# Expert stage of a two-layer diffusion backbone: routing tables, normed rows and final gathers moved

## The chip, the cores and the metric

The kernel runs on one core of one Trainium2 chip. The metric is the device time of one launch in microseconds (us). Before the change three runs gave 2681.62, 2683.39 and 2692.31 us; the median, 2683.39 us, is the time before.

## What is computed

The reference is a two-layer backbone over 512 latent tokens and 256 context tokens, with 1024 channels in fp32. Each layer has a modulated RMSNorm, four token mixers, an output projection with a gated residual, then a second modulated norm and a feed-forward part. The change touches the feed-forward part of the last layer, which sends each token to two of eight experts:

```python
h2 = rms_norm(x_lat, norm2_g) * (1.0 + sc2) + sh2
logits = h2 @ router
top_val, top_idx = lax.top_k(logits, 2)
gates = jax.nn.softmax(top_val)
out = sum over e of combine[..., e] * ((silu(h2 @ w1[e]) * (h2 @ w3[e])) @ w2[e])
x_lat = x_lat + g2 * out
return rms_norm(x_lat, final_norm_g)
```

An expert is 1024 to 1408 to 1024. Only the 512 latent tokens take part, so there are 1024 token-expert pairs.

## The kernel before

The program is traced in Python; a compile-time scheduler then fixes each engine's order, with the traced order as priority. An engine works strictly in its fixed order. Matrix products are made from fp32r parts: an operand is split into a high part (a ScalarE copy, L259) and a low part (a VectorE subtraction, L260), and `mm3` (L272 to L274) adds three products.

**Output projection with the router beside it.** The mixers' end multiplies by w_out in eight column tiles m. For the last layer `moe_begin` first loads the router and a table of constants (`mc`), and with `spread` (L319, L320: eight TensorE transposes and two ScalarE copies) lays the norm's scale `Ar` and the gate `g2r` out as rows. Then `moe_add` (L1640) makes each tile of the new x, and `moe_x` (L1643 on) adds to the sum of squares, adds to the router's logits and turns the tile into rows of tokens: x into `xt`, x times `Ar` into `hm`.

**`moe_route` (L1658 on).** From the sum of squares it takes each token's 1/rms, `rs`. ScalarE scales the four 128-row parts of `hm` by `rs` (L1677) and SP writes them to the DRAM tensor `hd` (L1678); SP also writes `xt` to `xq` (L1675). VectorE ranks the logits, counts tokens per expert and orders the experts by count, so that the three largest get two blocks of 128 tokens each ("wide") and the other five one block ("narrow"): NB = 11 blocks, and NOV = 4 more that are run only if a count overflows. The table of which token stands in which row of which block, `inv`, is written at L1765. After it stand the results' tables: the gates by way of an Exp on ScalarE (L1785), `gr` (each block row's gate, L1799 to L1801), `rowE` and `rowL` (where each token's two results will lie, L1812, L1813), and for the last block `li` and `g7` (token numbers, the other result's row, gate; L1848 to L1851). Their temporaries lie in the pool `mh`, whose space the expert stage takes over once it is closed.

**`moe_run` (L1854 on).** Two lanes share the stage: lane 0 has the three wide experts, lane 1 the five narrow ones. Each expert has 11 steps f, one for each 128 columns of the hidden layer, so lane 0 has 33 steps, lane 1 has 55, and 88 in all. A step loads 1.5 MB of weights on SP's queue into three buffers `rawm` and two `rawv`, splits them on ScalarE and VectorE, and multiplies: `first` makes silu(w1)*w3, and `second`, one step later in the order, adds its product with w2 to the block's result in PSUM. A wide step has 48 products of 256 columns and 12 of 512, a narrow one 24 and 6. The order of the steps is written out by hand:

```python
order = sorted(((i + 0.5) / len(t) * (0.87 if early and n == 0 else 1), n, *x) for n, t in enumerate(todo) for i, x in enumerate(t))
```

With 0.87 the wide lane ends early and the last seven steps are narrow, all of the last block (NB - 1). The first step is narrow, the second wide. POOL gathers a block's rows from `hd` by `inv` (`fetch`, L1864); `rows_in` turns them by eight transposes a block (L1877) in two PSUM tiles, and from each it makes four pairs of 128x128: ScalarE adds the shift `mB` and takes the high part (L1881), VectorE adds the shift and takes the low part (L1882). At f == 10 a block's result is multiplied by `gr` and `g2r` (L1938) and written by POOL to `yb` (L1939). The PSUM tag `sml`, with two buffers, serves the products of `first` and the transposes.

**The end.** Seven steps before the end `early` is traced: POOL gathers by `rowE` and `li` from `yb` with an add (L1970), four parts of `xt` twice and then the last block's rows `x7` (a tile `xr`) twice, and `norm_out` squares, normalizes and writes the four parts (L1977 to L1983). `final` does the same for the last block's own rows after the last product (L2016 to L2025). After that the overflow count is read and the conditional part is skipped when it is zero.

Of the kernel before, what the change touches and what calls it, by code (L numbers as in the profile page):

```python
# [11 lines left out]
F32 = mybir.dt.float32  # L12
# [210 lines left out]
class Ker:  # L223
# [1385 lines left out]
    def moe_begin(s, l, wp):  # L1609

        E, V, S, mh, mod = s.E, s.V, s.S, s.mh, s.mods[l]
        s.rt = mh.tile([128, KT, 8], F32, name="router")
        s.mc = mh.tile([128, 349], F32, name="mcst")
        s.Q.dma_start(s.rt, s.I['router'])
        s.Q.dma_start(s.mc, s.I['mcst'])
        A = mh.tile([128, KT], F32, name="mA")
        V.scalar_tensor_tensor(A, mod[:, 32:40, 0], 1.0, s.prm[:, l, P_N2:P_N2 + 8], op0=OP.add, op1=OP.mult)
        s.RA = mh.tile([128, KT, 8], F32, name="RA")
        V.tensor_mul(s.RA, s.rt, A[:, :, None].to_broadcast([128, KT, 8]))
        s.Ar = wp.tile([128, D], F32, name="Ar")  # L1620
        s.mB = mod[:, 24:32, 0]
        for dst, src in ((s.Ar, A), (s.g2r, mod[:, 40:48, 0])):
            s.spread(dst, src, s.tx)
        ps = s.tx()
        for k in range(KT):
            E.matmul(ps[:, :8], mod[:, 24 + k, 0:1].to_broadcast([128, 128]), s.rt[:, k], start=k == 0, stop=k == KT - 1)
        s.bR = mh.tile([128, 8], F32, name="bR")
        V.tensor_copy(s.bR, ps[:, :8])
        s.ltr, s.onr = (mh.tile([128, 128], F32R, name=n) for n in ("ltr", "onr"))
        V.tensor_copy(s.ltr, s.mc[:, 72:200])  # L1630
        V.tensor_copy(s.onr, s.ones)
        s.hm = mh.tile([128, 4, D], F32, name="hm")
        s.lgt = s.ps("lgt")
# [8 lines left out]
    def moe_x(s, m, wp):  # L1642

        x = s.xl[m]
        s.sumsq(m, LAT, wp, x)
# [9 lines left out]
    def moe_route(s, wp):  # L1655
# [15 lines left out]
        lg = tp.tile([128, 4, 8], F32, name="lg")  # L1671
        V.tensor_mul(lg, ps[:, :32].rearrange("p (a b) -> p a b", a=4), rs[:, :, None].to_broadcast([128, 4, 8]))
        V.tensor_add(lg, lg, s.bR[:, None].to_broadcast([128, 4, 8]))
        for j in range(4):
            s.Q.dma_start(s.xq[128 * j:128 * j + 128], s.xt[j])  # L1675
        for j in range(4):
            S.activation(s.hm[:, j], s.hm[:, j], AF.Copy, scale=rs[:, j:j + 1])  # L1677
            s.Q.dma_start(s.hd[128 * j:128 * j + 128], s.hm[:, j])  # L1678
# [11 lines left out]
        rk = tp.tile([128, 4, 8], F32, name="rk")  # L1690
# [11 lines left out]
        cnt = tp.tile([128, 1, 8], F32, name="cnt")  # L1702
        V.tensor_copy(cnt[:, 0], pq[:, :8])
        er = tp.tile([128, 1, 8], F32, name="er")
# [8 lines left out]
        w = tp.tile([128, 8, 8], F32, name="ew")  # L1713
# [26 lines left out]
        rf = tp.tile([128, 2, 4], F32, name="rf")  # L1740
        one = [tp.tile([128, 4, 8], F32, name=f"one{i}") for i in range(2)]
# [7 lines left out]
        ge = tp.tile([128, 8, 17], F32, name="ge")  # L1749
        V.tensor_tensor(ge, rr[:, :, None].to_broadcast([128, 8, 17]), mc[:, None, 200:217].to_broadcast([128, 8, 17]), OP.is_ge)  # L1750
        pl = tp.tile([128, 8], F32, name="pl")
# [6 lines left out]
        ohp = tp.tile([128, 8, 128], F32R, name="ohp")  # L1758
# [18 lines left out]
        V.tensor_copy(s.regv, ef[0:1, 8:13])  # L1777

# [12 lines left out]
        gh, gl = (tp.tile([128, 8, 2, 16], F32R, name=f"g{n}") for n in "hl")  # L1791
        gh, gl = gh[:, :, 0], gl[:, :, 0]
# [4 lines left out]
        pg = s.tx()  # L1797
# [48 lines left out]
        p7 = s.tx()  # L1846
# [6 lines left out]
    def moe_run(s, lanes, wp, early=None, final=None):  # L1853
# [14 lines left out]
        def rows_in(blocks, xrs):  # L1868
# [4 lines left out]
            for i, xr in enumerate(xrs):  # L1873
                for q in range(2):
                    ps = s.sml()
                    for k in range(4):
                        E.transpose(ps[:, 128 * k:128 * k + 128], xr[:, 512 * q + 128 * k:512 * q + 128 * k + 128], s.idn)  # L1877
                    for k in range(4):
                        o = (slice(None), 4 * q + k, slice(128 * i, 128 * i + 128))
                        pk, m = ps[:, 128 * k:128 * k + 128], s.mB[:, 4 * q + k:4 * q + k + 1]  # L1880
                        S.activation(a[o], pk, AF.Identity, bias=m)  # L1881
                        V.scalar_tensor_tensor(c[o], pk, m, a[o], op0=OP.add, op1=OP.subtract)  # L1882
# [60 lines left out]
        order = sorted(((i + 0.5) / len(t) * (0.87 if early and n == 0 else 1), n, *x) for n, t in enumerate(todo) for i, x in enumerate(t))  # L1943
# [5 lines left out]
        for at, (_, n, j, f) in enumerate(order):  # L1949
# [15 lines left out]
            if early and at == len(order) - 7:  # L1965
                early()
# [18 lines left out]
    def moe(s):  # L1985
# [6 lines left out]
        with s.pool("pr", 1, PSUM) as s.pp:  # L1992
            s.nsml = 2
            with s.pool("mw") as wp:
                fo = wp.tile([128, 8], F32, name="fos")

                def early():
# [29 lines left out]
                s.moe_run([[(expert(j), [2 * j, 2 * j + 1]) for j in range(3)], [(expert(j), [3 + j]) for j in range(3, 8)]], wp, early, final)  # L2027
# [6 lines left out]
            with s.tc.If(nov > 0):  # L2034
# [5 lines left out]
                with s.pool("fin") as fp:  # L2040
# [3 lines left out]
                    s.norm_out(fp, fp.tile([128, 4], F32, name="fss"))  # L2044
# [39 lines left out]
```

## Time and profile before

| | |
|---|---|
| median of three runs | 2683.39 us |
| the profiled execution's own time | 2689.9 us |
| its span, first to last instruction | 2688.1 us |
| TensorE busy | 2423.1 us, 90% |
| VectorE, ScalarE, POOL busy | 62%, 46%, 18% |
| transfers | 327.73 MB, 122 GB/s over the span |

The profile gives one execution's instructions. Busy time of TensorE is pipelined, so that a full row need not be the engine's peak. PEclk is the TensorE clock that was granted, as a share of 2.4 GHz: 1.00 and 0.50 are its two levels. "DMA share" is the busy share of the core's 16 DMA engines. A timeline row has start, duration, engine, line and operands (out<-in), and in brackets the idle time before it with what ended it. "Landing" is the time from a transfer's issue to its data's arrival.

### The profile page before, as it was taken

What the parts mean: (1) busy time and instruction counts of PE and PEld (TensorE: products, weight loads), DVE (VectorE), ACT (ScalarE), POOL (GpSimd) and SP (SyncE); (2) the same over time, 40 slices, a digit from 0 to 9 for tenths busy, and PEclk for the clock granted to TensorE, in tenths of its full rate; (3) what the DMA queues carried; (4) which work ended last, traced back from release to release, by engine and by line L of the source; (5) the groups of instructions that cost most, each with busy time, mean ns of one, the idle gap of its engine ahead of it and who ended that gap; (6) DMA issues with size and microseconds to landing.
All of it is one profiled execution on the core that took longest, in us unless ns stands there. A gap on an engine that the chain in (4) does not pass through costs nothing. (4 is left out here: it accounts for less than half of the span.)

```text
span 2688.1 us, 46555 instructions
## 1 busy us (share of the span) xinstructions
PE 2423.1 (90%) x18148; PEld 2005.0 (75%) x18148; DVE 1661.6 (62%) x3158; ACT 1240.9 (46%) x2396; POOL 483.9 (18%) x619
## 2 busy tenths in 40 slices
PE   7999788879988999999999998888995989999993
PEld 3889666656677888888887876765674979988882
DVE  5573698877497544343355738876635676667673
ACT  3373366546623211212234726754734565655552
POOL 1010454541020000000120025653011000000011
PEclk9999898999999999999999999999996999999996
DMA  6233100011054434343411320001126877878785
GB/s 239 75 96 112 50 25 27 22 64 56 24 169 153 128 104 126 112 131 126 130 44 60 94 71 2 25 27 47 40 66 223 266 255 247 263 235 267 235 280 159
DMA packets 162037, 327.73 MB, mean 122 GB/s; under 512 B 12400, under 2 KB 84848, under 8 KB 161808
## 3 DMA queue, kind: packets, MB, share of 16 engines
q1 hardware_dynamic: 153600, 294.65, 34.1%
q0 software_dynamic: 8208, 30.02, 3.6%
q8 instruction: 145, 2.38, 0.4%
q14 instruction: 84, 0.69, 0.1%
HBM read 296.97 MB, written 26.21 MB: 120 GB/s over the span
## 5 line engine op out<-in xcount | busy, mean ns | idle before, releaser
L272 PE MATMUL big<-hhi,hiw 128*128 128x512 f32 (+1 forms) x1504 | 519.4, 346 | 8.1 <-ACT hhi L491 3.5
L273 PE MATMUL big<-hlo,hiw 128*128 128x512 f32 (+1 forms) x1504 | 521.5, 347 | 2.4 <-DVE hlo L492 2.4
L274 PE MATMUL big<-hhi,low 128*128 128x512 f32 (+1 forms) x1504 | 517.7, 344 | 5.6 <-DVE low L260 3.9
L259 ACT CAST hiw<-raww 128x512 fp32r<-128x512 f32 (+3 forms) x208 | 158.4, 769 | 612.4 <-PE big L273 408.2
L272 PEld LDWEIGHTS big<-hhi,hiw 128*128 128x128 f32 x1504 | 285.0, 190 | 52.4 <-ACT hhi L491 5.4
L274 PEld LDWEIGHTS big<-hhi,low 128*128 128x128 f32 x1504 | 284.5, 189 | 45.2 <-DVE low L260 5.6
L273 PEld LDWEIGHTS big<-hlo,hiw 128*128 128x128 f32 x1504 | 285.2, 190 | 41.3 <-DVE hlo L492 4.2
L260 DVE TENSOR_TENSOR lom<-rawm,him 128x1024 fp32r<-128x1024 f32 x176 | 214.9, 1224 | 128.6 <-ACT him L259 126.5
L260 DVE TENSOR_TENSOR low<-raww,hiw 128x512 fp32r<-128x512 f32 (+3 forms) x196 | 177.1, 908 | 158.2 <-ACT hiw L259 157.9
L259 ACT CAST him<-rawm 128x1024 fp32r<-128x1024 f32 x176 | 183.9, 1046 | 149.0 <-PE sml L273 63.9
L272 PE MATMUL sml<-xh,him 128*128 128x256 f32 x528 | 154.0, 292 | 0.2
L273 PE MATMUL sml<-xl,him 128*128 128x256 f32 x528 | 151.7, 287 | 0.0
L274 PE MATMUL sml<-xh,lom 128*128 128x256 f32 x528 | 151.5, 287 | 0.0
L272 PE MATMUL sml<-him,xh 128*128 128x256 f32 x440 | 129.0, 293 | 10.0 <-DVE xl L1882 9.0
L260 DVE TENSOR_TENSOR lov<-rawv,hiv 128x1024 fp32r<-128x1024 f32 x88 | 107.5, 1221 | 47.4 <-ACT hiv L259 46.0
L273 PE MATMUL sml<-lom,xh 128*128 128x256 f32 x440 | 127.2, 289 | 0.0
L274 PE MATMUL sml<-him,xl 128*128 128x256 f32 x440 | 127.0, 289 | 0.0
L273 PE MATMUL big<-gl,hiw 128*128 128x512 f32 (+1 forms) x352 | 119.5, 339 | 0.0
L259 ACT CAST hiv<-rawv 128x1024 fp32r<-128x1024 f32 x88 | 92.2, 1048 | 58.5 <-PE y L274 48.4
L272 PE MATMUL big<-gh,hiw 128*128 128x512 f32 (+1 forms) x352 | 118.9, 338 | 0.0
L274 PE MATMUL big<-gh,low 128*128 128x512 f32 (+1 forms) x352 | 118.2, 336 | 0.0
L757 POOL TENSOR_TENSOR Gm<-G,mskf 128x256 f32<-128x256 f32 x120 | 98.9, 832 | 82.3 <-PE a L612 79.0
(610 smaller groups left out, 5676.8 us busy)
## 6 DMA issues: line engine op xcount, KB each, us to landing
rawm<-in_m SPq DMA_DIRECT2D x176, 512.0 KB, 5.1
rawv<-in_m SPq DMA_DIRECT2D x88, 512.0 KB, 5.0
raww<-in_wadt SPq DMA_DIRECT2D x56, 512.0 KB, 3.5
raww<-in_w SPq DMA_DIRECT2D x52, 512.0 KB, 3.9
raww<-in_winc SPq DMA_DIRECT2D x92, 256.0 KB, 3.0
raww<-in_wout SPq DMA_DIRECT2D x16, 512.0 KB, 4.2
wadt<-in_wadt SPq DMA_DIRECT2D x16, 512.0 KB, 4.3
raww<-in_w SPq DMA_DIRECT2D x16, 448.0 KB, 3.3
```

The source lines that it names most:

```text
L259: s.S.copy(hi, src)
L260: (eng or s.V).tensor_sub(lo, src, hi)
L272: s.E.matmul(out, ah, bh, start=start, stop=False)
L273: s.E.matmul(out, ah, bl, start=False, stop=False)
L274: s.E.matmul(out, al, bh, start=False, stop=stop)
L757: P.tensor_mul(x, G[:, :, 0, :, 0], s.mskf[:, 1 - d, i][:, None, None].to_broadcast(sh))
```

## The change

- `hd` is filled with the shift `sh2` before the rows exist: in `moe_begin` the buffer `g2r` holds the spread shift first, and SP writes it to the four parts of `hd`. In `moe_route` the scaled `hm` is added to `hd` by four POOL transfers with `accum_op=add`; the four writes of `xq` are traced after them. The gate is spread into `g2r` later, in `moe_x` at m == 4.
- `rows_in` no longer adds the shift: one ScalarE copy and one VectorE subtraction for 128x512 take the place of four pairs of 128x128.
- The results' tables become `moe_tables`, traced as a hook after step 2 of the 88, with their PSUM from `sml`; the tiles that they read or make are moved to the pool `mo`, which stays open.
- The wide lane's factor is 0.8, so that eleven narrow steps are last. The gathers (`sums`) are traced eleven steps before the end, with `x7`'s gather after the four of each round; `norm_out` is split: the squares (`norm_rms`) three steps before the end, two parts of the output two steps before, and two one step before.

```diff
-        s.mc = mh.tile([128, 349], F32, name="mcst")
+        s.mc = s.mo.tile([128, 349], F32, name="mcst")
...
-        s.mB = mod[:, 24:32, 0]
-        for dst, src in ((s.Ar, A), (s.g2r, mod[:, 40:48, 0])):
+        for dst, src in ((s.Ar, A), (s.g2r, mod[:, 24:32, 0])):
             s.spread(dst, src, s.tx)
+
+        for j in range(4):
+            s.Q.dma_start(s.hd[128 * j:128 * j + 128], s.g2r)
...
+        if m == 4:
+            s.spread(s.g2r, s.mods[1][:, 40:48, 0], s.tx)
...
         for j in range(4):
+            S.activation(s.hm[:, j], s.hm[:, j], AF.Copy, scale=rs[:, j:j + 1])
+            P.dma_start(s.hd[128 * j:128 * j + 128], s.hm[:, j], accum_op=OP.add)
+        for j in range(4):
             s.Q.dma_start(s.xq[128 * j:128 * j + 128], s.xt[j])
-        for j in range(4):
-            S.activation(s.hm[:, j], s.hm[:, j], AF.Copy, scale=rs[:, j:j + 1])
-            s.Q.dma_start(s.hd[128 * j:128 * j + 128], s.hm[:, j])
 
         def rank(dst, x, n):
...
-        ohp = tp.tile([128, 8, 128], F32R, name="ohp")
+        ohp = s.mo.tile([128, 8, 128], F32R, name="ohp")
...
+        s.tab = lg, one, ge, pl, ohp, rf, er, cnt, u
+
+    def moe_tables(s):
+
+        E, V, S, tp, mc = s.E, s.V, s.S, s.mo, s.mc
+        lg, one, ge, pl, ohp, rf, er, cnt, u = s.tab
+        y = tp.tile([128, 4, 8], F32, name="yl")
...
-        pg = s.tx()
+        pg = s.sml()
...
-                    for k in range(4):
-                        o = (slice(None), 4 * q + k, slice(128 * i, 128 * i + 128))
-                        pk, m = ps[:, 128 * k:128 * k + 128], s.mB[:, 4 * q + k:4 * q + k + 1]
-                        S.activation(a[o], pk, AF.Identity, bias=m)
-                        V.scalar_tensor_tensor(c[o], pk, m, a[o], op0=OP.add, op1=OP.subtract)
+                    pv = ps.rearrange("p (a b) -> p a b", a=4)
+                    o = (slice(None), slice(4 * q, 4 * q + 4), slice(128 * i, 128 * i + 128))
+                    s.split(a[o], c[o], pv)
...
-        order = sorted(((i + 0.5) / len(t) * (0.87 if early and n == 0 else 1), n, *x) for n, t in enumerate(todo) for i, x in enumerate(t))
+        order = sorted(((i + 0.5) / len(t) * (0.8 if final and n == 0 else 1), n, *x) for n, t in enumerate(todo) for i, x in enumerate(t))
...
-            if early and at == len(order) - 7:
-                early()
+            for f in hooks.get(at, ()) + hooks.get(at - len(order), ()):
+                f()
...
-    def norm_out(s, fp, ss):
-
-        V, S = s.V, s.S
+    def norm_rms(s, fp, ss):
+
         for j in range(4):
-            S.activation(fp.tile([128, D], F32, name="fo", bufs=2), s.xt[j], AF.Square, accum_out=ss[:, j:j + 1])
-        S.activation(ss, ss, AF.Sqrt, bias=s.epsc[:, 0:1], scale=1.0 / D)
-        V.reciprocal(ss, ss)
-        for j in range(4):
+            s.S.activation(fp.tile([128, D], F32, name="fo", bufs=2), s.xt[j], AF.Square, accum_out=ss[:, j:j + 1])
+        s.S.activation(ss, ss, AF.Sqrt, bias=s.epsc[:, 0:1], scale=1.0 / D)
+        s.V.reciprocal(ss, ss)
+
+    def norm_out(s, fp, ss, js=range(4)):
+
+        for j in js:
             o = fp.tile([128, D], F32, name="fo", bufs=2)
-            V.scalar_tensor_tensor(o, s.xt[j], ss[:, j:j + 1], s.fng, op0=OP.mult, op1=OP.mult)
+            s.V.scalar_tensor_tensor(o, s.xt[j], ss[:, j:j + 1], s.fng, op0=OP.mult, op1=OP.mult)
...
-                def early():
+                def sums():
...
                             s.gather(s.xt[j], s.yb, s.rowE[:, i, j:j + 1], True)
-                    for i in range(2):
                         s.gather(x7, s.yb, s.li[:, 1 + i:2 + i], True)
-                    s.norm_out(s.mraw, fo[:, :4])
                     V.tensor_scalar_mul(late['G'], s.g2r, s.g7)
...
-                s.moe_run([[(expert(j), [2 * j, 2 * j + 1]) for j in range(3)], [(expert(j), [3 + j]) for j in range(3, 8)]], wp, early, final)
+                s.moe_run([[(expert(j), [2 * j, 2 * j + 1]) for j in range(3)], [(expert(j), [3 + j]) for j in range(3, 8)]], wp,
+                          {2: (s.moe_tables,), -11: (sums,), -3: (lambda: s.norm_rms(s.mraw, fo[:, :4]),),
+                           -2: (lambda: s.norm_out(s.mraw, fo, (0, 1)),), -1: (lambda: s.norm_out(s.mraw, fo, (2, 3)),)}, final)
```

## Rows read from the trace of the kernel before

**Rows 1.** Stage start, windows: busy us by engine (instructions), PEclk, DMA share, GB/s

```profile
2020.00:2025.00 5.00, 1.13 (x6) 1.04 (x5) 4.31 (x38) 2.12 (x2) 0.00 (x0) 0.50 1.03 403
...
2050.00:2055.00 5.00, 0.85 (x4) 0.85 (x5) 1.96 (x4) 1.94 (x4) 0.00 (x0) 0.50 0.80 324
```

**Rows 2.** Stage start, POOL timeline: start us, us, instruction, idle before

```profile
2039.34 1.07 POOL L1864 DMA_INDIRECT xr<-hd,inv  x1 [30.83 <-DVE g L1851]
```

**Rows 3.** Same stretch, VectorE in order of time

```profile
2030.03 0.17 DVE L1765 CAST inv<-tx 128x15 int32<-128x15 f32 x1 [0.91 <-PE tx L1764]
...
2038.53 0.15 DVE L1851 TENSOR_REDUCE g<-tx 128x1 f32<-128x2 f32 x1
```

**Rows 4.** Same stretch, TensorE in order of time

```profile
2032.61 0.38 PE L1799 MATMUL tx<-gh,ohp 128*128 128x16 f32 x1 [2.61 <-DVE gh L1795]
...
2044.22 1.94 PE L1877 MATMUL sml<-cst,xr 128*128 128x128 f32 x8 [5.81 <-issue]
2054.15 0.58 PE L272 MATMUL sml<-him,xh 128*128 128x256 f32 x1 [7.99 <-DVE xl L1882]
...
2069.83 0.58 PE L272 MATMUL sml<-xh,him 128*128 128x256 f32 x1
```

**Rows 5.** Same stretch, ScalarE in order of time: the scaling of the normed rows

```profile
2016.55 4.30 ACT L1677 ACTIVATE hm<-hm,mrs 128x1024 f32<-128x1024 f32 x4
```

**Rows 6.** Same stretch, DMA issues: KB each, median us to landing

```profile
hd<-hm SPq DMA_DIRECT2D x4, 512.0 KB, 5.8
```

**Rows 7.** Kernel end, transfers of tile xm: 8 accumulating gathers, 4 plain writes

```profile
DMA to landing us min/median/max: 6.0/12.2/15.1
```

**Rows 8.** Steady stage, 2075 to 2598 us, groups by line: busy us, mean ns, idle before

```profile
L1881 ACT ACTIVATE xh<-sml,mod 128x128 fp32r<-128x128 f32 x64 | 21.6, 365 | 15.6 <-DVE xl L1882 13.6 <-PE sml L1877 2.0
L1882 DVE SCALAR_TENSOR_TENSOR xl<-sml,mod,xh 128x128 fp32r<-128x128 f32 x64 | 20.5, 346 | 8.9 <-ACT xh L1881 8.9
```

**Rows 9.** A 128x512 PSUM read on ScalarE and one on VectorE, before the stage

```profile
1951.43 0.58 ACT L1103 COPY PT<-pt 128x512 f32<-128x512 f32 x1
...
1979.90 0.69 DVE L1651 TENSOR_TENSOR hm<-tx,Ar 128x512 f32<-128x512 f32 x1 [0.55 <-PE tx L1649]
```

**Rows 10.** Steady stage, 53 stretches of 10 us, two of them and the sum

```profile
2210.00:2220.00 10.00, 5.53 (x27) 4.15 (x26) 6.36 (x17) 5.56 (x15) 1.98 (x2) 0.79 0.60 197
...
2390.00:2400.00 10.00, 6.75 (x27) 5.30 (x26) 5.68 (x15) 5.32 (x15) 1.98 (x2) 0.50 0.57 193
...
sum 530.00, PE 508.69 PEld 467.51 DVE 358.99 ACT 307.84 POOL 16.79; mean PE 9.60 PEld 8.82 DVE 6.77 ACT 5.81 POOL 0.32
```

**Rows 11.** Steady stage, SP queue: weight loads two steps apart

```profile
2480.73 3.21 SPq L264 DMA_DIRECT2D rawm<-in_m  x2
...
2493.60 3.42 SPq L264 DMA_DIRECT2D rawm<-in_m  x2
```

**Rows 12.** Output projection, TensorE: the spread of a row of the modulation

```profile
1965.64 1.19 PE L319 MATMUL tx<-cst,mod 128*128 128x128 f32 x8
```

**Rows 13.** End of the kernel, in order of time, VectorE, then POOL, then ScalarE

```profile
2597.86 2.72 DVE L1938 SCALAR_TENSOR_TENSOR xm<-y,gr,g2r 128x512 f32<-128x512 f32 x4
...
2608.03 1.66 POOL L1970 DMA_INDIRECT xm<-yb,rowE  x1 [6.61 <-DMA yb<-xm]
...
2645.95 2.38 POOL L1970 DMA_INDIRECT xr<-yb,li  x1 [12.15 <-DMA xr<-yb,li]
...
2674.94 1.01 POOL L2025 DMA_INDIRECT out<-fo,li  x1 [15.46 <-DVE fo L2024]
...
2634.00 1.06 ACT L1977 ACTIVATE fo<-xm 128x1024 f32<-128x1024 f32 x1 [16.54 <-DMA xm<-yb,rowE]
...
2642.30 1.06 ACT L1977 ACTIVATE fo<-xm 128x1024 f32<-128x1024 f32 x1 [0.57 <-DMA xm<-yb,rowE]
```

**Rows 14.** End of the kernel, by stretches, columns as in rows 1

```profile
2600.00:2605.00 5.00, 5.00 (x38) 4.74 (x37) 4.03 (x6) 3.00 (x4) 1.18 (x3) 1.00 1.00 369
2605.00:2610.00 5.00, 4.97 (x36) 4.35 (x35) 3.88 (x6) 3.26 (x7) 1.67 (x2) 1.00 0.93 342
```

More of the change, by code (lines that the diff above doesn't have):

```diff
@@ L1670, in moe_route @@
             E.transpose(ps[:, 8 * j:8 * j + 8], lgs[:, 128 * j:128 * j + 128], s.idn[:8, :8])
-        lg = tp.tile([128, 4, 8], F32, name="lg")
+        lg = s.mo.tile([128, 4, 8], F32, name="lg")
         V.tensor_mul(lg, ps[:, :32].rearrange("p (a b) -> p a b", a=4), rs[:, :, None].to_broadcast([128, 4, 8]))
@@ L1689, in rank @@
             V.tensor_reduce(dst, gt, AX.X, OP.add)
-        rk = tp.tile([128, 4, 8], F32, name="rk")
+        rk = s.mo.tile([128, 4, 8], F32, name="rk")
         rank(rk, lg, 4)
@@ L1701, in moe_route @@
             E.matmul(ps[:, 8 * d:32], s.onr, sf[:, :32 - 8 * d], start=False, stop=d == 3)
-        cnt = tp.tile([128, 1, 8], F32, name="cnt")
+        cnt = s.mo.tile([128, 1, 8], F32, name="cnt")
         V.tensor_copy(cnt[:, 0], pq[:, :8])
-        er = tp.tile([128, 1, 8], F32, name="er")
+        er = s.mo.tile([128, 1, 8], F32, name="er")
         rank(er, cnt, 1)
@@ L1712, in moe_route @@
         V.tensor_copy(regs, ef[0:1, :8])
-        w = tp.tile([128, 8, 8], F32, name="ew")
+        w = s.mo.tile([128, 8, 8], F32, name="ew")
         nb, big, base, cap, ov, ob, u = (w[:, i] for i in range(7))
@@ L1739, in moe_route @@
         V.tensor_tensor(t, t, base[:, None].to_broadcast(sh), OP.add)
-        rf = tp.tile([128, 2, 4], F32, name="rf")
-        one = [tp.tile([128, 4, 8], F32, name=f"one{i}") for i in range(2)]
+        rf = s.mo.tile([128, 2, 4], F32, name="rf")
+        one = [s.mo.tile([128, 4, 8], F32, name=f"one{i}") for i in range(2)]
         y = tp.tile([128, 4, 8], F32, name="yy")
@@ L1748, in moe_route @@
         rr = rf.rearrange("p a b -> p (a b)")
-        ge = tp.tile([128, 8, 17], F32, name="ge")
+        ge = s.mo.tile([128, 8, 17], F32, name="ge")
         V.tensor_tensor(ge, rr[:, :, None].to_broadcast([128, 8, 17]), mc[:, None, 200:217].to_broadcast([128, 8, 17]), OP.is_ge)
-        pl = tp.tile([128, 8], F32, name="pl")
+        pl = s.mo.tile([128, 8], F32, name="pl")
         V.tensor_reduce(pl, ge[:, :, 1:], AX.X, OP.add)
@@ L1790, in moe_route @@
         gg = tp.tile([128, 8, 16], F32, name="gg")
-        gh, gl = (tp.tile([128, 8, 2, 16], F32R, name=f"g{n}") for n in "hl")
-        gh, gl = gh[:, :, 0], gl[:, :, 0]
+        gh, gl = (tp.tile([128, 8, 16], F32R, name=f"g{n}") for n in "hl")
         for i in range(2):
@@ L1845, in moe_route @@
         V.tensor_copy(oh0, c7[:, 0:1].to_broadcast([128, 128]))
-        p7 = s.tx()
+        p7 = s.sml()
         for i in range(8):
@@ L1851, in moe_route, with moe_run @@
         V.tensor_reduce(s.g7, p7[:, 3:5], AX.X, OP.add)
-    def moe_run(s, lanes, wp, early=None, final=None):
+    def moe_run(s, lanes, wp, hooks={}, final=None):
         E, V, S, P = s.E, s.V, s.S, s.P
@@ L2043, in moe @@
                             s.gather(s.xt[j], s.yb, s.rowL[:, i, j:j + 1], True)
-                    s.norm_out(fp, fp.tile([128, 4], F32, name="fss"))
+                    ss = fp.tile([128, 4], F32, name="fss")
+                    s.norm_rms(fp, ss)
+                    s.norm_out(fp, ss)
     def run(s):
```

## The prediction

> **What bounds the kernel now.** I read the page first (the table above): TensorE is busy for 90% of the span, so time can be won only where it is idle. The stretches of the windows then show two such places, one on each side of the expert stage; I took the timelines of both, engine by engine, and last the steady stage between them.
>
> The first place is the stage's start. TensorE works 1.13 of 5 us and then 0.85 of 5 us, at a granted clock of 0.50, its level of 1.2 GHz [rows 1]. The chain that ends last there is read in three steps. POOL waits 30.83 us, until 2039.34, to gather the first rows, and what released it is VectorE's last write of the tables, at 2038.53 [rows 2, 3]. The gather itself needs only `inv`, which was there at 2030.03 [rows 3]. TensorE turns the rows from 2044.22, but the first product, of a narrow step, starts at 2054.15, having waited 7.99 us for a pair of `rows_in`, and the first wide product at 2069.83 [rows 4]. ScalarE had scaled the normed rows by 2020.85 [rows 5].
>
> The second place is the end, for which see part C; the steady stage is between them.
>
> **A, the start.** Four edits go together here.
>
> *Normed rows.* The four scalings end at 2016.55 + 4.30 = 2020.85 [rows 5]. The plain writes of `hd` landed 5.8 us after issue [rows 6]. No accumulating write to DRAM is in this trace. From below it is bounded by the plain write: 2020.9 + 5.8 = 2026.7, earlier than `inv`. From above it is bounded by the slowest accumulating gather, 15.1 us [rows 7]: 2036.0. I take the median of that row, 12.2, because it mixes plain writes and accumulating gathers and because the DMA engines are saturated here (share 1.03 [rows 1]) as they were there: complete at 2033.1, gather at 2033.4, 5.9 us earlier (bounds 9.0, with `inv` as the limit, and 3.3).
>
> *Tables out of the way.* Nothing that the gather or the weights' split parts overlay is written by the tables any more, so the wait for 2038.53 goes; that is already in the 5.9. What is late next is the accumulated `hd`.
>
> *`rows_in`.* A pair costs 365 ns on ScalarE and 346 on VectorE [rows 8], and the two alternate. Per 128x512 tile one copy of 0.58 and one subtraction of 0.69 replace four pairs [rows 9]. Before, 9.9 us passed from the first transposes to the first product [rows 4]; now it is 1.94 for the transposes, the second half's 0.58 + 0.69, and 0.8 for splits of weights queued ahead on ScalarE, 4.0 in all: 5.9 us more. The wide step's sixteen pairs filled 15.7 us between the two first products [rows 4]; four copies and subtractions take 5.1, and lie beside the narrow product, so I leave 7.7 of it: 8.0 more (bounds 4 and 10). The wide step starts 5.9 + 5.9 + 8.0 = 19.8 us earlier.
>
> *What comes back.* The tables' 25 small products, their copies and an Exp now stand after step 2, on engines that follow a fixed order. From 2030.03 to 2038.53 they took 8.5 us [rows 3]; the products started at 2032.61 [rows 4] and so filled 5.9. I charge 6 (bounds 0, if other products fill the waits, and 8.5). They take the two `sml` buffers from the products, and `first` is queued behind them; that is in the upper bound. The accumulates read what they add to, 2 MB more; at 403 GB/s [rows 1] that is 5.2 us of saturated transfer, and the first weights come behind it. I charge 4 (bounds 0 and 8). On SP's queue the four writes of the shift stand ahead of the output projection's next weights; they land in about 5.8 us each, side by side [rows 6], well inside the stretch to the first gather, and the weights have buffers in front of them: nothing (bounds 0 and 2; with the buffers gone they would cost those 2).
>
> A = 19.8 - 6 - 4 = 9.8 us gained (bounds 9.0 + 5.9 + 10 = 25, and 3.3 + 4 + 4 - 8.5 - 8 = -5, with the narrow term at 4).
>
> **B, the steady stage.** TensorE is busy 508.69 of 530 us, so 21.3 are idle; the worst stretches, 5.53 and 6.75 of 10, are those where a wide `rows_in` runs, and there the granted clock also fell to 0.79 and 0.50 [rows 10]. Per tile the alternating pairs, 4 x 0.71 = 2.8 us, become 1.27, so 55% of that wait should go: 12 of 21. ScalarE and VectorE also split weights there, which does not change, so I take 8 (bounds 2 and 16).
>
> **C, the end.** A wide and a narrow step take 2493.60 - 2480.73 = 12.87 us [rows 11]; a narrow one has half of the products, so 4.3. Four more narrow steps leave the mixed part: the last sums can begin 17.2 us sooner, apart from A and B. Behind them are ten narrow steps instead of six.
>
> The extra spread is cheap and counted here for good: eight transposes, 1.19 us [rows 12], in a part where TensorE is full; D = -1 us (bounds -1 and -3, if its two ScalarE copies hold up a split).
>
> Now the tail before: from the last wide results (2597.86) to the last issue (2674.94) it took 77.1 us. In it ScalarE stood for 16.54 us, until 2634.00, in front of the first square, waiting for the gathers; no weights were split meanwhile. The squares then waited for one part after the other: (2642.30 - 2634.00) / 3 = 2.77 us a gather. The last of ten gathers was issued at 2645.95, 37.9 us after the first [rows 13]. Without gathers the weights came at 369 and 342 GB/s with share 1.00 and 0.93 [rows 14], 355 in the mean.
>
> After: weights of ten steps, 15.7 MB at 355 GB/s, 44.3 us; ten gathers at 2.77, 27.7; the results' write of 1 MB, 3; what is loaded already, some 1.5 steps, -6; the last step after its last load, with `final`, 14. In all 83 us, as the DMA engines are the bound and work on either. Against 77.1, and started 17.2 earlier: 11.3 gained. The squares no longer stand in front of casts for long, but now lie in the last three steps: four at 1.06 and two table loads, about 7 us of ScalarE work, of which I charge 4. C = 7.3. Bounds: were the tail again to leave the DMA engines idle for 12 us, -5; were TensorE's ten steps the bound (43 + 14 + 10 for the write = 67), 77.1 - 67 + 17.2 - 4 = 23.
>
> **Sum.** 9.8 + 8 + 7.3 - 1 = 24.1 us. Against the profiled run's own 2689.9 that makes 2665.8; it is 6.5 above the median of the three runs, and the same gain from 2683.4 gives **2659 us**.
>
> **Rivals.**
> 1. *The start is bound by transfers.* The wide step waits for its weights, and A is 0. For it: share 1.03 at 2020 [rows 1]. Against: the weights' split parts also waited for the tables, so loads move with them. 2683.4 - 14.3 = 2669.
> 2. *The tail gives nothing.* Eleven narrow steps share the DMA engines with the gathers and ScalarE still stands before the squares: C = -5, 2671. For it: the gathers alone kept the engines saturated. Against: with ten steps behind them there is work to hide them.
> 3. *The tail becomes TensorE's.* C = 23: 2644. For it: the weights' rate without gathers; against: 2.77 us a gather.
> 4. *POOL's issues are held up.* An issue took 1.07 us at 2039.34 but 2.38 at 2645.95 [rows 2, 13]. Beside the router's small VectorE operations four issues at 2.38 instead of 1.07 put `hd` 5.2 us later: 2664. The Trainium skill, page "SBUF — State Buffer", section "Who interferes with whom", says that VectorE copies, casts and tensor-scalar operations in a two-port mode shut GpSimd out of writing descriptors. By that rule this rival would hold; these rows show the longer issue, not its reason.
> 5. *Slower: the four accumulates go one behind the other*, as adds to one DRAM tensor. Then, from 2017.6, `hd` is complete at 2017.6 + 4 x 15.1 = 2078.0, 44.9 us after my 2033.1; the 4 us of late weights come back, and the time is 2659 + 41 = 2700. It decides from about 14.3 us for each (2697). For it: each is a read and a write of the tensor that the gather needs whole. Against: the parts are disjoint, and the plain writes overlapped.
>
> That the tables don't move off the path at all is in rival 1.
>
> **How the numbers follow.** Chances: the forecast 0.50, rival 1 0.15, rival 2 0.12, rival 3 0.10, rival 4 0.05, rival 5 0.08. About 0.5%, 13.4 us, is what a measurement of this kernel tells from no change; so faster is below 2670.0 and slower above 2696.8. Faster: 0.48 of the forecast's, rivals 3 and 4, and 0.05 of rival 1: 0.68. Slower: rival 5, 0.08. The rest, 0.24, is no change. The range leaves out rival 5 and the ends of the bounds: 2640 to 2676.
>
> **What would show it.** Right: POOL's first gather near 2033 on this time scale, released by the accumulates; the first wide product near 2050; no idle of 5 us in 10 beside `rows_in`; ScalarE without a 16 us stand at the squares, and the time from the last wide results to the last issue near 87 us. Wrong: a first gather after 2039, the tables' products with long idle before them, or DMA shares of 1.0 from the gathers' first to last with steps of more than 9 us.

## The result, and the profile after

The median fell from 2685.2 to 2656.6 us (four runs of each), a ratio of 0.989 (95% interval 0.987 to 0.992). The forecast was 2659. The sum held, in part by luck: of its terms one was far too small and two too large.

All marks below are counted from the last residual tile (VectorE's last `xl` of `moe_add`), 2012.41 us before and 2009.38 after. A POOL subtraction of line 260 ahead of everything that the change touches started at 1910.20 before and 1906.25 after, so 3.95 us of the two profiles' difference lie outside the change. The marks themselves are 3.03 us apart, so the extra spread cost 3.95 - 3.03 = 0.9.

The start after, timelines of POOL, TensorE; these answer [rows 2 to 4].

```profile
2015.00 2.91 POOL L1680 DMA_DIRECT2D hd<-hm  x3 [9.82 <-ACT hm L1679]
2018.09 0.85 POOL L1680 DMA_DIRECT2D hd<-hm  x1 [0.18 <-issue]
2034.68 1.06 POOL L1874 DMA_INDIRECT xr<-hd,inv  x1 [15.74 <-DMA rawv<-in_m]
...
2039.83 1.94 PE L1887 MATMUL sml<-cst,xr 128*128 128x128 f32 x8 [12.92 <-DMA xr<-hd,inv]
2042.32 0.58 PE L272 MATMUL sml<-him,xh 128*128 128x256 f32 x1 [0.55 <-DVE xl L260]
...
2055.08 0.28 PE L272 MATMUL sml<-xh,him 128*128 128x256 f32 x1
```

The first gather came 25.3 us after the last residual tile (26.9 before), the first product, of a narrow step, at 32.9 (41.7), the first wide one at 45.7 (57.4). The bracket of POOL's gather names a weight load, which the gather doesn't read. The chain that ended last names the last accumulate, ahead of ScalarE's first cast:

```profile
2009.38 0.76 DVE xl L1642
...
2018.09 15.12 DMA hd<-hm
2033.62 1.05 ACT him L259
...
2036.74 8.19 DMA rawv<-in_m
```

That accumulate landed at 2018.09 + 15.12 = 2033.21, and the gather, which reads `hd`, started 1.5 us later. In E5 below the last one was issued at 2017.54 and landed within 13.3 us, and the gather started at 2032.29, again 1.5 us behind. ScalarE's first cast of weights waited for the same transfer, as its tile lies over `hm`. Then the windows after, with columns as in [rows 1]: two stretches of the start, the steady stage from the first wide product to the last wide results, the emptiest of its stretches of 10 us (counted from 2055), and two of the end.

```profile
2020.00:2025.00 5.00, 0.00 (x0) 0.00 (x0) 4.97 (x41) 0.00 (x0) 0.00 (x0) 0.50 1.05 232
2025.00:2030.00 5.00, 1.85 (x8) 1.78 (x8) 2.29 (x18) 0.00 (x0) 0.00 (x0) 0.50 1.05 256
2055.08:2548.48 493.40, 484.27 (x3396) 448.12 (x3395) 332.16 (x416) 280.61 (x394) 13.76 (x20) 1.00 0.81 256
2185.00:2195.00 10.00, 7.14 (x47) 5.79 (x45) 7.03 (x10) 5.92 (x10) 0.93 (x1) 1.00 0.95 317
2580.00:2585.00 5.00, 3.31 (x13) 2.82 (x13) 1.42 (x2) 0.28 (x2) 2.42 (x2) 0.54 1.05 274
2585.00:2590.00 5.00, 0.00 (x0) 0.00 (x0) 0.00 (x0) 0.00 (x0) 2.71 (x2) 0.50 1.06 275
```

While the accumulates run, and from 2021.94 the first weights with them, ScalarE stands, TensorE works 0.00 and 1.85 of 5 us, and the DMA engines are full at 232 and 256 GB/s (403 before at nearly the same share [rows 1]). In the steady stage the mean clock is 1.00, and the emptiest stretch holds 7.14 of 10 us of products at 1.00 (before, 5.53 and 6.75 at 0.79 and 0.50 [rows 10]). At the end TensorE stands again, with the DMA engines full. The end in order of time, VectorE, POOL, ScalarE; these answer [rows 13]:

```profile
2548.48 2.72 DVE L1946 SCALAR_TENSOR_TENSOR xm<-y,gr,g2r 128x512 f32<-128x512 f32 x4
...
2562.13 1.72 POOL L1978 DMA_INDIRECT xm<-yb,rowE  x1 [5.24 <-DMA yb<-xm]
...
2588.38 1.55 POOL L1978 DMA_INDIRECT xr<-yb,li  x1 [2.22 <-DMA xr<-yb,li]
...
2640.72 1.01 POOL L2033 DMA_INDIRECT out<-fo,li  x1 [9.35 <-DVE fo L2032]
...
2580.01 0.27 ACT L1915 ACTIVATE mt<-sml 128x128 f32<-128x128 f32 x1
2591.99 1.06 ACT L1984 ACTIVATE fo<-xm 128x1024 f32<-128x1024 f32 x1 [11.71 <-DMA xm<-yb,rowE]
```

The ten gathers are issued in 26 us instead of 38, but ScalarE still stands 11.71 us ahead of the first square. On ScalarE that square comes right behind the activation of 2580.01, although it is traced four steps later. From the last wide results to the last issue it took 92.2 us (77.1 before); by the forecast's 4.3 us a step, 17.2 of that are the four narrow steps that moved here. E1, which moves them back, has a wide stage that is 18.7 us longer.

### The profile page after: what moved, and what is told of

It is laid out like the page before. It is cut to its first block, busy times and chain, and to the rows that moved or that the text cites. A ratio compares the mean times of both kernels' runs of the same rounds, so it can differ in the third digit from the quotient of the medians.

```text
span 2654.2 us, 46437 instructions
## 1 busy us (share of the span) xinstructions
PE 2416.8 (91%) x18156; PEld 2006.9 (76%) x18156; DVE 1647.2 (62%) x3092; ACT 1225.4 (46%) x2332; POOL 484.1 (18%) x623
## 3 DMA queue, kind: packets, MB, share of 16 engines
HBM read 296.97 MB, written 28.31 MB: 123 GB/s over the span
## 5 line engine op out<-in xcount | busy, mean ns | idle before, releaser
L272 PE MATMUL sml<-him,xh 128*128 128x256 f32 x440 | 130.7, 297 | 15.1 <-ACT him L259 14.5
```

The costliest lines, as they stand in the source:

```text
L272: s.E.matmul(out, ah, bh, start=start, stop=False)
```

## The experiments

One table for all, worked out from the start times of the same rows as above in each kernel's trace. The first three columns are counted from the last residual tile. "Wide stage" runs from the first wide product to the last wide results, "end" from there to the last issue, and "sum" from the last residual tile to the last issue. In all rows but before, E1 and E9 the end holds four narrow steps more. Ratios are to the kernel before on the same chip, with 95% intervals.

| kernel | first gather | first product | first wide | wide stage | end | sum | ratio |
|---|---|---|---|---|---|---|---|
| before | 26.9 | 41.7 | 57.4 | 528.0 | 77.1 | 662.5 | 1 |
| changed | 25.3 | 32.9 | 45.7 | 493.4 | 92.2 | 631.3 | 0.989 (0.987, 0.992) |
| E1 end undone | 25.3 | 32.9 | 45.7 | 512.1 | 76.1 | 633.9 | 0.990 (0.988, 0.992) |
| E2 tables undone | 25.7 | 33.3 | 48.4 | 492.4 | 91.9 | 632.8 | 0.988 (0.986, 0.990) |
| E3 plain hd | 18.2 | 27.7 | 40.6 | 496.2 | 90.4 | 627.2 | 0.987 (0.984, 0.989) |
| E4 rows_in undone | 18.6 | 32.5 | 50.9 | 515.9 | 90.4 | 657.3 | 0.998 (0.997, 0.999) |
| E5 xq late | 23.5 | 31.1 | 42.1 | 494.9 | 90.1 | 627.0 | 0.988 (0.986, 0.991) |
| E6 shift in rows_in | 18.2 | 27.7 | 38.3 | 499.5 | 89.9 | 627.6 | 0.986 (0.984, 0.988) |
| E7 squares late | 25.6 | 33.5 | 47.7 | 496.5 | 94.3 | 638.5 | 0.992 (0.990, 0.994) |
| E8 = E4, tables undone | 18.6 | 32.3 | 50.0 | 510.4 | 90.3 | 650.7 | 0.996 (0.995, 0.998) |
| E9 before + rows_in | 26.9 | 34.2 | 47.6 | 506.9 | 76.3 | 630.8 | 0.987 (0.985, 0.990) |
| E10 = E6, tables undone | 18.6 | 29.0 | 39.1 | 490.6 | 91.2 | 620.9 | 0.983 (0.981, 0.986) |
| E11 = E6, xq late | 18.6 | 25.7 | 39.7 | 494.7 | 91.0 | 625.3 | 0.984 (0.982, 0.986) |
| E12 = E10, xq late | 18.6 | 29.6 | 40.7 | 490.1 | 90.7 | 621.4 | 0.985 (0.983, 0.987) |

How far one profile can be trusted is in the table too: up to the first wide product the changed kernel, E1 and E7 run the same program, and it comes at 45.7, 45.7 and 47.7; the wide stage, which E7 doesn't change either, took 493.4 and 496.5. So one profile doesn't tell a difference of 3 us in one part, or of 5 us in a sum.

**E1, the end undone.**

```diff
-        order = sorted(((i + 0.5) / len(t) * (0.8 if final and n == 0 else 1), n, *x) for n, t in enumerate(todo) for i, x in enumerate(t))
+        order = sorted(((i + 0.5) / len(t) * (0.87 if final and n == 0 else 1), n, *x) for n, t in enumerate(todo) for i, x in enumerate(t))
...
+                    for i in range(2):
                         s.gather(x7, s.yb, s.li[:, 1 + i:2 + i], True)
+                    s.norm_rms(s.mraw, fo[:, :4])
+                    s.norm_out(s.mraw, fo)
...
-                          {2: (s.moe_tables,), -11: (sums,), -3: (lambda: s.norm_rms(s.mraw, fo[:, :4]),),
-                           -2: (lambda: s.norm_out(s.mraw, fo, (0, 1)),), -1: (lambda: s.norm_out(s.mraw, fo, (2, 3)),)}, final)
+                          {2: (s.moe_tables,), -7: (sums,)}, final)
```

> The changed kernel with its end as it was before (factor 0.87, ten gathers, squares and results traced together seven steps ahead of the end); start and rows_in stay changed. Theory (the new trace: from the last wide results to the last issue 92.2 us against 77.1, with 17.2 of it only moved from the mixed part): the end is worth about 2 us, so this kernel is 1 to 4 us slower than the changed one, about 26 us under the kernel before, ratio 0.990. Rival (the forecast's term C): the end is worth 7.3, ratio 0.992; and if the end is worth nothing or loses, this kernel is as fast as the changed one or faster, 0.989 or below. In the profile, first wide product to last issue: changed kernel 585.6 us; here 587 to 589 by the theory, 593 by the rival.

Measured: from first wide product to last issue 512.1 + 76.1 = 588.2 against 585.6. By this the end was worth 2.6 us, not 7.3; neither the ratios nor one profile can tell it from nothing.

**E2, the tables in the router's part again** (`moe_tables` joined to `moe_route`, PSUM from `tx`).

> The changed kernel with the results' tables computed in the router's part again, ahead of the stage (their tiles stay in the pool that nothing overlays). Theory: the first gather is set by the accumulates on hd, at 25.3 us after the last residual tile, not by the tables, and TensorE is idle there until 32; so the tables' 25 products fit ahead of the first turned rows, the first gather stays within 1 us of 25.3 and the total within 2 us of the changed kernel. Rival (the forecast): the tables block POOL or TensorE there for 6 to 8.5 us, first turned rows and first wide product that much later, ratio about 0.9915.

Measured: first gather 25.7, sum 1.5 us more than the changed kernel: no difference that can be told. In this kernel the theory held; but see E8 and E10, where `hd` is written plainly.

**E3, hd written plainly.** The shift is left out of the computation.

```diff
-            P.dma_start(s.hd[128 * j:128 * j + 128], s.hm[:, j], accum_op=OP.add)
+            s.Q.dma_start(s.hd[128 * j:128 * j + 128], s.hm[:, j])
```

> The changed kernel with the normed rows written to hd plainly by SP; the shift is left out of the computation (no first write of it, no second spread, no accumulate). Theory: four accumulates that take 15 us hold the first gather; with plain writes (5.8 us each, side by side, behind xq) it is bound by inv and starts 19 to 20 us after the last residual tile instead of 25.3; the first wide product comes 5 to 6 us earlier (40 instead of 45.7), and the total is 5 to 7 us below the changed kernel (1 of it the spread), ratio 0.987. Rival: the start is bound by the transfer of the first weights (DMA share near 1 from 2013 to 2034); then the first gather is early but the first wide product moves by 2 us at most, ratio 0.9885.

The first gather and both first products, in its POOL and TensorE timelines:

```profile
2028.50 1.06 POOL L1870 DMA_INDIRECT xr<-hd,inv  x1 [22.11 <-DVE vb L1838]
...
2038.03 0.58 PE L272 MATMUL sml<-him,xh 128*128 128x256 f32 x1 [0.81 <-ACT him L259]
...
2050.89 0.39 PE L272 MATMUL sml<-xh,him 128*128 128x256 f32 x1
```

Measured: first gather 7.1 us sooner than with accumulates and 1.1 behind `inv` (2027.41), first wide product 5.1 sooner. The accumulates cost some 5 us at the start; rival 1's bound, the transfer of the first weights, did not set in.

**E4, rows_in undone on top of E3.** This also brings the shift back.

```diff
-                    pv = ps.rearrange("p (a b) -> p a b", a=4)
-                    o = (slice(None), slice(4 * q, 4 * q + 4), slice(128 * i, 128 * i + 128))
-                    s.split(a[o], c[o], pv)
+                    for k in range(4):
+                        o = (slice(None), 4 * q + k, slice(128 * i, 128 * i + 128))
+                        pk, m = ps[:, 128 * k:128 * k + 128], s.mB[:, 4 * q + k:4 * q + k + 1]
+                        S.activation(a[o], pk, AF.Identity, bias=m)
+                        V.scalar_tensor_tensor(c[o], pk, m, a[o], op0=OP.add, op1=OP.subtract)
```

> As the run with plain writes of hd, and rows_in as before: per 128x512 tile four pairs of a biased copy and a subtraction that add the shift (nothing is left out of the computation). Theory: the gain of 17 us between the first wide product and the last wide results comes from rows_in, as TensorE's waits there fell from 21 to 9 us; here that stretch is 12 to 17 us longer than in the run with plain writes (493 becomes 505 to 510), the first wide product 8 to 10 us later, in all 20 to 27 us more, ratio about 0.996. Rival (the forecast's B = 8, the rest of the gain from the interleaving and the clock): the stretch is 6 to 9 us longer, in all 14 to 17 us, ratio about 0.993.

The wide stage of E4 in its windows:

```profile
2062.96:2578.90 515.94, 494.90 (x3399) 455.40 (x3398) 341.83 (x465) 293.02 (x446) 14.69 (x21) 0.97 0.76 244
```

and of E3:

```profile
2050.89:2547.10 496.21, 486.54 (x3395) 450.47 (x3396) 334.00 (x417) 280.88 (x394) 13.91 (x21) 0.99 0.80 257
```

Measured: 30.1 us more than E3 in the sum, more than even the theory said: 10.4 at the first wide product and 19.7 in the wide stage. The wide stage has the same number of products; 11.4 us of the 19.7 are idle time (515.94 - 494.90 against 496.21 - 486.54), and 8.4 are products that took longer, at a mean clock of 0.97 instead of 0.99.

**E5, xq's writes behind the first weights.**

```diff
+            V.scalar_tensor_tensor(s.xt[j][:, :1], s.g7, 0.0, s.xt[j][:, :1], op0=OP.mult, op1=OP.add)
             s.Q.dma_start(s.xq[128 * j:128 * j + 128], s.xt[j])
```

(moved from `moe_route` to the end of `moe_tables`; the addition makes them wait.)

> The changed kernel with the four plain writes of xq (2 MB) moved behind the first weights on SP's queue (each made to wait for the tables' last result). Theory: the accumulates take 15 us because they share the DMA engines (share 1.0 from 2013) with xq's writes; without them hd is complete 3 to 5 us sooner, the first gather comes 20.5 to 22.5 us after the last residual tile instead of 25.3, the first wide product 3 to 5 us sooner, ratio about 0.988. Rival: an accumulating write to DRAM is that slow by itself; then the first gather stays within 1.5 us of 25.3 and only the weights come sooner, no change of the total.

Transfers of tile `hd` from 2013 to 2019, then two windows and SP's first weight loads, of E5:

```profile
DMA to landing us min/median/max: 5.1/9.1/13.3
```

```profile
2015.00:2020.00 5.00, 1.32 (x8) 1.26 (x8) 4.48 (x41) 3.74 (x5) 2.94 (x4) 0.63 0.90 148
2018.00:2020.00 2.00, 0.00 (x0) 0.00 (x0) 1.97 (x21) 0.76 (x2) 0.39 (x1) 0.50 1.14 197
...
2021.32 1.53 SPq L264 DMA_DIRECT2D rawm<-in_m  x2
```

In the changed kernel the same view says

```profile
DMA to landing us min/median/max: 8.2/11.2/15.1
```

Measured: the first gather moved by 1.8 us only. Both stories fell short: the sharing with `xq` makes 2 us, while the accumulates fill the DMA engines (share 1.14 at 197 GB/s) even before weights are asked for. The weights came sooner (first wide product by 3.6), and the sum fell by 4.3, which neither the ratio nor one profile tells from the changed kernel.

**E6, the shift added by VectorE in rows_in, on top of E3.**

```diff
+                    t = wp.tile([128, 4, 128], F32, name="xsh", bufs=2)
+                    V.tensor_tensor(t, pv, s.mB[:, 4 * q:4 * q + 4, None].to_broadcast([128, 4, 128]), OP.add)
-                    s.split(a[o], c[o], pv)
+                    s.split(a[o], c[o], t)
```

> The changed kernel without accumulates: hd is written plainly by SP, and rows_in adds the shift with one VectorE addition of a 128x512 tile ahead of the copy and the subtraction; no second spread. Nothing is left out of the computation. Theory: the price of the accumulates at the start is 5 us and that of twenty more VectorE additions of 0.7 us is hidden except in the first tiles: first gather 18 us after the last residual tile, first wide product 42 to 43 (45.7 in the changed kernel, 40.6 with plain writes), the stretch to the last wide results 493 to 498, total 2 to 4 us below the changed kernel, ratio 0.988. Rival: VectorE becomes what TensorE waits for in rows_in again; the stretch grows to 502 or more and the total is 3 us or more above the changed kernel, ratio 0.991.

Measured: sum 627.6, 3.7 under the changed kernel, with the whole computation. The theory's total held, its parts less so: the first wide product came at 38.3 (42 to 43 expected), and the wide stage, 499.5, lies between the theory's and the rival's.

**E7, squares later.**

```diff
+                    V.tensor_scalar_mul(fo[:, 7:8], s.cur[:, 0:1], 0.0)
+                    s.norm_rms(s.mraw, fo[:, :4], fo[:, 7:8])
```

(`s.cur` is the last `mt`, the added operand the squares' bias; hook -5 in place of -3.)

> The changed kernel with the four squares tied to a later step (their bias is 0 times a value of the step five ahead of the end), so that ScalarE goes on casting weights and doesn't stand 11.7 us for the gathers. Theory: the DMA engines bound the end (share 1.03 to 1.06 from 2565 to 2600 with the gathers); weights that are asked for sooner only take their share from the gathers, and the time from the last wide results to the last issue stays within 3 us of 92.2. Rival: the stand of ScalarE is what costs, as no weights are split and TensorE is idle from 2583 to 2594; then 6 to 10 us are gained, 82 to 86 us, ratio 0.986.

ScalarE's waits of E7 from 2555 to 2665 us, those of the changed kernel from 2548 to 2645, then four windows of E7's end:

```profile
ACT him L259 <- DMA rawm<-in_m: 22.1, 12, 2.8
...
ACT hiv L259 <- DMA rawv<-in_m: 7.1, 3, 2.6
```

```profile
ACT him L259 <- DMA rawm<-in_m: 14.9, 10, 2.9
ACT fo L1984 <- DMA xm<-yb,rowE: 12.5, 3, 11.7
...
ACT hiv L259 <- DMA rawv<-in_m: 1.4, 2, 1.1
```

```profile
2585.00:2590.00 5.00, 0.63 (x3) 0.38 (x3) 2.29 (x3) 1.22 (x2) 2.58 (x2) 1.00 1.04 273
2595.00:2600.00 5.00, 2.97 (x13) 2.30 (x11) 1.30 (x2) 2.20 (x3) 1.89 (x1) 0.78 1.05 274
2615.00:2620.00 5.00, 3.64 (x16) 3.05 (x15) 1.37 (x2) 4.98 (x11) 0.00 (x0) 0.50 0.90 362
2620.00:2625.00 5.00, 3.33 (x8) 1.94 (x8) 3.64 (x6) 4.96 (x7) 0.60 (x1) 0.50 0.13 51
```

Measured: no stand at the squares any more, and the end 94.3 us, as the theory said. ScalarE now waits for the weights instead, with the DMA engines as full as before: its waits for transfers come to 22.1 + 7.1 = 29.2 us, and to 14.9 + 12.5 + 1.4 = 28.8 in the changed kernel. By this the stand of 11.7 us was a part of what the transfers cost, and not a cost of its own. It isn't shown cleanly, though: the four squares now follow one another on ScalarE, which is full from 2615 to 2625, while the DMA share falls to 0.13. What that took back is not known. The other 5 us of E7's 7 lie in parts whose program is unchanged.

**E8, tables undone on top of E4.**

> As the run with rows_in as before, and the tables computed in the router's part too: of the change only the tables' place in memory, the end and its interleaving are left. Theory: where the tables are computed is worth little, since their products fit into TensorE's idle time ahead of the first turned rows and only their place in memory held the gather back; first gather within 2 us of 18.6 after the last residual tile, first wide product within 3 us of 50.9, total within 3 us of that run, ratio 0.998. Rival (the forecast's start): tables ahead of the stage hold the first gather or the first products by 6 to 8.5 us, first wide product at 57, ratio 1.001.

POOL's first gather and two VectorE rows of E8, the writes of `inv` and of the tables' last result:

```profile
2023.91 1.06 POOL L1866 DMA_INDIRECT xr<-hd,inv  x1 [22.52 <-DMA rawm<-in_m]
...
2022.82 0.17 DVE L1766 CAST inv<-tx 128x15 int32<-128x15 f32 x1 [0.81 <-PE tx L1765]
...
2030.33 0.15 DVE L1853 TENSOR_REDUCE g<-tx 128x1 f32<-128x2 f32 x1
```

Measured: first gather 18.6 as in E4, but the sum 6.6 us less, more than the theory's 3. The gather started 1.1 us behind `inv` and 6.4 ahead of the tables' last result, which it had waited for before. So its 27 us before came from where the tables' tiles lay and not from when they were computed; beside the first products the tables cost up to 6.6 us here.

**E9, the kernel before with rows_in alone** (E6's three lines in it, nothing else).

> The kernel before with rows_in alone changed: per 128x512 tile one VectorE addition of the shift, one copy and one subtraction in place of four pairs; tables, plain writes of hd and the end as before. Theory: rows_in alone carries most of the change. First gather still 27 us after the last residual tile (the tables' memory), first wide product 10 us sooner than before (47 instead of 57.4), the stretch to the last wide results 510 to 516 instead of 528, the end 77 as before; from the last residual tile to the last issue 634 to 641 us instead of 662.5, ratio about 0.991. Rival (the forecast's B = 8): the stretch is 520, as the idle of 21 us falls by 8 and the clock's part in it stays; 644 us, ratio 0.993.

The wide stage of the kernel before, which [rows 10] showed in other stretches, and one of these again with the one after it:

```profile
2069.83:2597.86 528.03, 506.72 (x3494) 465.63 (x3495) 356.85 (x483) 306.60 (x465) 15.82 (x23) 0.98 0.77 251
...
2220.00:2230.00 10.00, 10.00 (x71) 9.73 (x71) 4.81 (x7) 5.20 (x9) 0.00 (x0) 0.87 0.39 118
```

E9's, with the second worst of its stretches of 10 us:

```profile
2053.47:2560.35 506.88, 498.21 (x3498) 461.25 (x3497) 358.40 (x450) 296.18 (x415) 17.84 (x23) 1.00 0.81 263
2190.00:2200.00 10.00, 8.73 (x64) 7.61 (x64) 8.84 (x13) 5.05 (x8) 3.01 (x2) 1.00 0.93 314
```

Its groups of `rows_in`, which answer [rows 8]:

```profile
L260 DVE TENSOR_TENSOR xl<-xsh,xh 128x512 fp32r<-128x512 f32 x16 | 10.8, 683 | 0.5 <-ACT xh L259 0.5
L1881 DVE TENSOR_TENSOR xsh<-sml,mod 128x512 f32<-128x512 f32 x16 | 10.8, 683 | 0.7 <-PE sml L1877 0.7
L259 ACT CAST xh<-xsh 128x512 fp32r<-128x512 f32 x16 | 9.7, 620 | 4.5 <-DVE xsh L1881 4.5
```

Measured: sum 630.8, under the theory's 634 to 641 and as good as the whole change (631.3). The wide stage is 21.15 us shorter with as many products: 12.6 less idle (21.31 to 8.67) and 8.5 from products that no longer run at the lower clock. In the kernel before the clock falls in the stretch where `rows_in` stalls TensorE and stays below 1.00 in the next, in which TensorE is busy all the time (0.87); in E9 it is 1.00 even in its emptiest stretches (8.71 and 8.73 of 10). The windows can price this: 1 - granted clock, summed over stretches of 10 us of the wide stage, is 9.8 us before and 0.8 in E9 (13.2 in E4 and 5.1 in E3). The differences, 9.0 and 8.1, come near the 8.5 and 8.4 by which the products got shorter. How full a stretch is does not fix its clock: the changed kernel has 7.14 of 10 us at 1.00 (above), and 8.28 at 0.83 from 2275 to 2285. VectorE has no less to do (21.6 us in these groups against 20.5 [rows 8]). What went are the waits of the two engines for each other, 15.6 and 8.9 us before, 4.5 and 1.2 now, and more than half of ScalarE's work (21.6 us before, 9.7 now); no run separates these two.

**E10, E11, E12: versions with the whole computation.** E10 is E6 with the tables undone as in E2, E11 is E6 with xq late as in E5, E12 is both, with xq tied to a value of the third step.

> The shift added by VectorE in rows_in, plain writes of hd, and the tables computed in the router's part again with their tiles in their new place. Theory: the tables' products (3 to 5 us of TensorE) fit into the idle time before the first turned rows, so leaving the stage they are worth 1 to 5 us: from the last residual tile to the last issue 622 to 627 us (627.6 with the tables beside the first products), ratio 0.985. Rival: as the first gather is now at 18 us and the first turned rows at 25, the tables come in the way of these on VectorE and TensorE; first wide product 3 us or more later than 38.3, total 628 to 632, ratio 0.987.

> The shift added by VectorE in rows_in, plain writes of hd, and the writes of xq moved behind the first weights. Theory: without accumulates the first gather is bound by inv, so it stays at 18 us after the last residual tile; the weights come sooner, which gives 0 to 2 us at the first products; total within 2 us of the run with xq in its place (627.6 us from the last residual tile to the last issue), ratio 0.986. Rival: the first weights bound the first products; then 3 to 5 us are gained, 623 to 625, ratio 0.9845.

> The shift added by VectorE in rows_in, plain writes of hd, tables in the router's part in their new place, and the writes of xq moved behind the first weights (tied to a value of the third step). Theory: the two gains go together in part, since tables and late xq both act on the stretch between the first gather (18.6 us after the last residual tile) and the first products; from the last residual tile to the last issue 617 to 621 us (620.9 with xq in its place, 625.3 with the tables beside the first products), ratio 0.982. Rival: with the weights there sooner the tables on VectorE and TensorE bound the first turned rows, and late xq gives nothing: 621 to 624 us, ratio 0.9835.

Measured: ratios 0.983, 0.984 and 0.985 against the changed kernel's 0.989. All three are lower, though E12's interval still touches that of the changed kernel, and among themselves they can't be told apart. E10's theory held in kind, with a gain above its 1 to 5 us (sum 620.9 against E6's 627.6). In E11 the first product came 2 us sooner, the first wide one not, and the sum, 625.3, lies between the theory's and the rival's. In E12 the rival held: xq late gives nothing on top.

## Why the prediction was right in sum and wrong in its terms

**A, the start: 9.8 forecast, 6.5 to 8 measured.** The first wide product moved 11.7 us instead of 19.8. The step that failed first is the landing of the accumulates: I took the median of the gathers' row, 12.2, and the last took 15.1, my upper bound. The gather then started 1.5 us behind the landing, where I had put 0.3, so it came 1.6 us earlier instead of 5.9. Without accumulates (E3) it comes 7.1 us sooner than that, 1.1 behind `inv`. The other step is the wide half of `rows_in`: by E9 `rows_in` gave 7.6 us up to the first product (5.9 forecast), but only 2.3 more to the wide one (8.0). In the changed kernel's chain a wait for weights (8.19 us from 2036.74) reaches 2.6 us into that stretch, and casts of weights, splits of rows and the transposes fill the rest.

Of what I charged, the 4 for transfers lie inside the 11.7, and no run separates them. The 6 for the tables are not settled. E1's wide stage, with the steps mixed as in E9's, is 512.1 us against 506.9, so 5.2 more; with 17.2 us for the four narrow steps the changed kernel's is 510.6, so 3.7 more. Undoing the tables gave nothing that can be told in the changed kernel (E2), and 6.6 and 6.7 us where `hd` is written plainly (E8, E10). Rival 1 was half right: transfers bind the start, but the accumulates' own up to the gather, and the weights' only in part behind it. Rival 5 fell, as the four land side by side in 8.2 to 15.1. Rival 4 fell too: the accumulates' issues took 0.85 to 0.92 us each, with VectorE busy for 4.07 of the 5 us from 2015. The rule of the Trainium skill (page "SBUF — State Buffer", section "Who interferes with whom") is not shown by this trace.

**B, the steady stage: 8 forecast, 21 measured (E9).** E9 adds the shift on VectorE instead of in the transfer; in the changed kernel the stage got 528.0 - 17.2 - 493.4 = 17.4 us shorter, with the tables in it. This is the step that failed most. The 12 us of idle that I worked out were right (12.6); I cut them to 8 for the splits that stay, which had no row behind it. And I quoted the granted clocks of 0.79 and 0.50 [rows 10] without giving them a price. They were worth 8.5 us.

**C, the end: 7.3 forecast, 2.0 by the trace, 2.6 by E1.** The step that failed is the end's length, 83 us and 4 for the squares, measured as 92.2. I priced all weights at 355 GB/s and added the gathers; with the gathers running the DMA engines were full at 274 and 275 GB/s. E7, where ScalarE's stand is gone but its waits for transfers are as long in all, has no shorter end. What was measured lies between the forecast and rival 2. Rival 3 fell.

**D, the spread: 1 forecast, 0.9 measured.**

Together 11.7 + (528.0 - 17.2 - 493.4) + (77.1 + 17.2 - 92.2) - 0.9 = 30.3 us against 24.1 forecast, and 28.6 between the medians. That 2659 lies so near to 2656.6 is luck in part: B's shortfall made up for the excess of A and C, and the median before is 1.8 us higher with the fourth run. Of what was to be seen, the stretches of [rows 10] without half-idle windows came as told; the first gather, the first wide product (2058 on the old scale, not 2050) and the end (92, not 87) did not. One sign of being wrong was there: the DMA engines stayed full (0.94 to 1.06) from the first gather to the last, and the steps there took up to 17.9 us, from ScalarE's activation of 2580.01 to that of 2597.92.

## What to carry to other kernels

When a wait on the pacing TensorE is removed, price the clock with the idle time: sum (1 - granted clock) over the stall's stretch and the one behind it, since that was two fifths of what E9 gained in the wide stage. Where two engines alternate on small pieces, count their waits for each other beside their work, and make the pieces large first: here E9's three lines alone gave what the whole change gave. Before a constant is moved into an accumulating transfer, compare it with one more vector operation on an engine with time left. Here that was cheaper in each of three pairs, by 3.7, 11.9 and 1.7 us of the sum (E6 against the changed kernel, E10 against E2, E11 against E5), though only the second is clear of the noise of a profile.

## What the hardware showed unexpectedly

Accumulating transfers filled the DMA engines at about half the bytes of plain ones. With the four writes to `hd` alone, ahead of any weights and without `xq` (E5, 2018 to 2020), the share was 1.14 at 197 GB/s. Plain traffic had 403 at 1.03 [rows 1] and 369 at 1.00 [rows 14]. The accumulating gathers of the end had 275 at 1.06, with the last weights still landing (those issued at 2581.94 took 16.0 us). What the writes to `hd` read from their destination is not in that count: HBM read is 296.97 MB on the pages of both kernels, and written 26.21 MB before and 28.31 after, the 2.1 MB of the shift. Whether those reads alone fill the engines, no run here settles.

Moving an instruction in the traced order need not move it on its engine, which is the scheduler's doing and not the chip's: the squares, traced three steps before the end, stood four steps further ahead on ScalarE, and only a true dependency (E7) put them later.
